# A fifth 2x2 problem in the FFN, and two output groups that share PSUM banks

## The chip, the cores and the metric

The kernel runs on one core of one Trainium2 chip. The metric is device time in microseconds of one execution, 1881.71 us before the change (median of 3 runs, 1881.66 to 1881.78).

## The reference

Two layers of a post-norm encoder over 512 tokens of width 1024, in float32. Each layer has a token mixer (retention, chunked attention and differential attention, gated, merged and projected) and a SwiGLU FFN with 2816 inner columns. The change is in the FFN:

```python
u = jnp.einsum('bsd,df->bsf', x, w_ffn_in[l])
u_gate, u_up = jnp.split(u, 2, axis=-1)
ffn = jnp.einsum('bsf,fd->bsd', jax.nn.silu(u_gate) * u_up, w_ffn_out[l])
x = _layer_norm(DEEPNORM_ALPHA * x + ffn, ln2_g[l], ln2_b[l])
```

## The kernel before, in words

**Numbers.** A float32 operand is carried as a pair of float32r, high and low. ACT casts the high part and DVE subtracts to get the low part. A product of two pairs is three matmuls (`mm3`, L121 to L124). Weights are loaded in blocks of 1 MB into four staging buffers (`st`, queue SP); ACT casts `wh` (L259, plain blocks L154) and DVE subtracts `wl` (L260, L155) into three pairs of weight buffers (`AHEAD`, L48). A staging buffer is free for the next load when its `wl` is done.

**2x2 problems.** Most of the FFN's products are done as 2x2 block problems with seven products (m1, m2, y, x, v, g, h) in place of eight, each of 24 matmuls of 512 columns. The weight sums that they need come about in two ways. A `Chain` (L193) adds the next block of weights onto the one in the staging buffer by an accumulating DMA, which is issued by POOL (`more`, L178) after that buffer was split. A `Close` adds staged blocks with DVE (L233, L239) and needs one accumulating DMA ahead (`ahead_a`). Both load the block for g ahead of time: a plain load and, when it has landed, an accumulating one onto it (`ahead_c`). Written "p m1" and so on: problem p, product m1.

**FFN, first part.** The 22 inner tiles of 128 columns are made from x1, the layer-norm of the mixer's output, turned (`x1T`: eight pairs of 128 rows by 512 tokens). Four problems p, q, r, u (`u_fin`, L1272) make tiles 0 to 15: p is a Chain, the others are Closes. Tiles 16 to 21 are plain (`u_ffn`, `u_ffn_first`); 16 and 17 run first, on the first 256 tokens and then on the rest, because the last tokens' layer-norm is not yet through. `Quarters.sums` makes the sums of x1T (`s_x1`), and `s_natural` makes the untransposed x1 on DVE. `s_turn` transposes the gated results back (eight PE transposes each, L1222).

**FFN, second part.** Two output groups o and w (`fout_items`, L1307) are Chains over hidden tiles 0 to 7 and 8 to 15. The left-hand sums are made by `Twins`: `ready` (m1, m2), `difference` (y), `sums` (x, v), `rest` (g, h), each a DVE operation or none and a split. Each product stands in PSUM for the two row blocks (j = 0, 1), and DVE adds it into z (`plus`, L1303) for each of o and w. Products x, g and h of a group accumulate onto the bank of m1, and v onto that of y. `fout_rest(0)` and `fout_rest(1)` add the products of the six plain tiles 16 to 21; the second runs to the layer's end with the layer-norm behind it.

**Order.** The items of the FFN stand in a list written by hand (L1364 to L1376). With each item stand groups of side work, which are run between the halves of the item. A scheduler orders the instructions of each engine when the kernel is built; on the chip every engine's queue runs in order.

Of the kernel before, what the change touches and what calls it, by code (L numbers as in the profile page):

```python
# [17 lines left out]
P = 128  # L18
# [3 lines left out]
KT = D // P  # L22
# [34 lines left out]
def trunk(ctx, tc, x_in, xT_in, w_in, ret_norm_g, da_norm_g, lq1, lk1, lq2, lk2, w_a, w_b, w_c, b_merge, w_out,  # L57
# [19 lines left out]
    def g(dt=F32, name="g"):  # L77
        return gp.tile([P, 512], dt, tag="g", name=name)
# [4 lines left out]
    def bank(name="ps"):  # L83
        return psp.tile([P, 512], F32, tag="ps", name=name)

    class Pair:


        def __init__(self, name="pr"):
            self.hi = g(F32R, name + "h")  # L90
            self.lo = g(F32R, name + "l")

    class HalfPair:

# [21 lines left out]
    def split(pr, src, cols=slice(None), scale=None):  # L116

        part_hi(pr.hi[:, cols], src, scale)
        part_lo(pr.lo[:, cols], src, pr.hi[:, cols], scale)

    def mm3(ps, lh, ll, rh, rl, start, stop, onto=False):  # L121
        nc.tensor.matmul(ps, lh, rh, start=start, stop=False, skip_group_check=onto)  # L122
        nc.tensor.matmul(ps, lh, rl, start=False, stop=False, skip_group_check=onto)  # L123
        nc.tensor.matmul(ps, ll, rh, start=False, stop=stop, skip_group_check=onto)  # L124
# [137 lines left out]
    class Quarters:  # L262
# [13 lines left out]
        def put(self, name, pr, sl):  # L276
            self.use[name] = pr.hi[:, sl], pr.lo[:, sl]

        def sums(self, t1, t2, scale=None):
            a, b = self.A, self.B  # L280
            sa, sb = g(name="sa"), g(name="sb")
            nc.vector.tensor_sub(sa[:, a], t1[:, b], t2[:, b])
            nc.vector.tensor_sub(sa[:, b], sa[:, a], t1[:, a])
            nc.vector.tensor_add(sb[:, a], t2[:, a], sa[:, b])
            nc.vector.tensor_sub(sb[:, b], t1[:, a], t1[:, b])
            p12, p43 = Pair("s12"), Pair("s43")
            split(p12, sa, scale=scale)
            split(p43, sb, scale=scale)
            for name, pr, sl in (("y", p12, a), ("x", p12, b), ("v", p43, a), ("g", p43, b)):
                self.put(name, pr, sl)  # L290

    class Twins:

# [33 lines left out]
        def rest(self):  # L327
            nc.vector.tensor_sub(self.a21, self.a11, self.a21)
            self.part("g", self.a21)
            self.part("h", self.a22)  # L330

    def product(acts, name, j, wt, ps=None):

# [26 lines left out]

    def proj_N(act, wts, t, ps, k0=0, start=True, stop=True):

        sl = slice(P * t, P * t + P)
        rows = [(wt, k) for wt in wts for k in range(wt.nk)]
        for i, (wt, k) in enumerate(rows):
            a = act[k0 + i]
            mm3(ps, a.hi[:, sl], a.lo[:, sl], wt.hi[:, k], wt.lo[:, k], start and i == 0, stop and i == len(rows) - 1)

    def rows_of(w, c, k0=0, nk=KT):

# [232 lines left out]
    def layer(l):  # L603
# [118 lines left out]
        def s_q(k):  # L722

            def fn():
                xq[k].sums(xf.pop(k), xf.pop(k + 4))
            return fn

        def u_two(hv, acts, left_done, right_done):
# [433 lines left out]
        def u_out1(*wts):  # L1162
            n = x1["n"]
            for t in range(NT):
                ps = bank("po")
                proj_N(mg, wts, t, ps)
                if t >= 1:
                    n.transposes(t - 1)
                residual(n.z[t][1], ps)
                n.stats(t, 1)  # L1170
                n.normalise(t)
                if t == 2:
                    n.to_T(0)

        banks0 = []
        for i in range(2):
# [49 lines left out]

        twins = {}

        def s_ready(gi, fp):
            def fn():  # L1230
                pa, pc, k = 2 * gi, 2 * gi + 1, 8 * gi + 2 * fp
                tw = twins[gi, fp] = Twins(half.pop((pa, 0, fp)), half.pop((pa, 1, fp)))
                tw.ready(half.pop((pc, 0, fp)))
                hid[k], hid[k + 1] = tw.each
            return fn

        def s_differ(gi, fp):
# [9 lines left out]
        def s_rest(gi, fp):  # L1247
            def fn():
                twins.pop((gi, fp)).rest()
            return fn  # L1250

        def s_hid(*ids):
# [6 lines left out]
        def s_x1(k):  # L1259
            def fn():  # L1260
                if k == 0:
                    x1q.update({i: Quarters(x1T[i], x1T[i + 4]) for i in range(4)})
                x1q[k].sums(x1f.pop(k), x1f.pop(k + 4))
            return fn

        def s_natural(*ts):
# [10 lines left out]
        def u_ffn_first(ids):  # L1277
            def fn(*wts):
                n = len(ids)
                pg, pu = [bank("pt") for _ in range(n)], [bank("pt") for _ in range(n)]  # L1280
                proj_T_half0(x1T, [(wts[i], P * j, p[i]) for i in range(n) for j, p in enumerate((pg, pu))],
                             {KT // 2: lambda: (x1["n"].transposes(3), x1["n"].to_T(1))})
                for i in range(n):
                    proj_T(x1T, wts[i], 0, ps=pg[i], half=1)
                    proj_T(x1T, wts[i], P, ps=pu[i], half=1)
                    ffn_done(ids[i], pg[i], pu[i])
            return [ffn_spec(i) for i in ids], fn

        def u_ffn(i):
            def fn(wt):  # L1290
# [13 lines left out]
            if final:  # L1304
                x2["n"].stats(t, hf)

        def fout_items(gi):  # L1307

            r0, kh = GROUPS[gi]
            hv = Chain(w_ffn_out[l], r0, kh)  # L1310
            w = {}

            def it(name, *adds):
# [12 lines left out]

            add, sub = ALU.add, ALU.subtract
            return {"c": hv.ahead_c, "m1": it("m1", (0, 0, add)), "y": it("y", (1, 1, add)), "x": it("x", (0, 1, sub)),
                    "m2": it("m2", (0, 0, add)), "v": it("v", (0, 1, add)), "g": it("g", (1, 1, sub)), "h": it("h", (1, 0, add))}

        def fout_rest(hf):

# [31 lines left out]
        for (specs, fn), *groups in [  # L1364
            (u_ffn_first([16, 17]), [s_natural(0)], [s_x1(0)]), (p["m1"], [s_x1(1)], [s_x1(2)]),
            (u_ffn(18), [s_x1(3), s_natural(1)], [p["c"]]), (p["m2"], [s_natural(2)], [s_natural(3)]), (p["y"],),
            (p["v"], [q["a"]]), (u_ffn(19),), (p["x"],), (q["m1"],), (p["g"],), (q["y"], [s_turn(0, 0)]), (p["h"], [q["c"]]),
            (q["v"], [r["a"]]), (q["m2"], [s_turn(0, 1)]), (q["x"],), (r["m1"],), (q["g"],), (r["y"], [s_turn(1, 0)]), (q["h"], [r["c"]]),
            (r["v"], [u["a"]]), (r["m2"], [s_turn(1, 1)]), (r["x"],), (u["m1"],), (r["g"],), (u["y"], [s_turn(2, 0)]),
            (r["h"], [u["c"]], [s_ready(0, 0)]), (u["v"], [s_ready(0, 1)]), (u["m2"], [s_turn(2, 1)]), (u["x"],),  # L1370
            (o["m1"], [s_differ(0, 0)], [s_differ(0, 1)]), (u["g"],), (o["m2"], [s_sums(0, 0)], [o["c"]]), (u["h"], [s_turn(3, 0)]),
            (o["y"], [s_sums(0, 1)]), (u_ffn(20), [s_rest(0, 0)], [s_rest(0, 1)]), (o["v"], [s_turn(3, 1)]),
            (o["x"], [s_ready(1, 0)], [s_ready(1, 1)]),
            (w["m1"], [s_differ(1, 0)]), (o["g"], [s_differ(1, 1)], [w["c"]]), (w["m2"], [s_sums(1, 0)]), (o["h"], [s_sums(1, 1)]),
            (w["y"], [s_rest(1, 0)]), (u_ffn(21), [s_rest(1, 1)], [s_hid(16, 17, 18)]), (w["v"], [s_hid(19, 20, 21)]), (w["x"],),
            (fout_rest(0),), (w["g"],), (w["h"],), (fout_rest(1),),  # L1376
        ]:
            item(specs, fn, *groups)

# [58 lines left out]
```

## Time and profile before

| | us |
|---|---|
| median of 3 runs | 1881.71 |
| the profiled execution | 1881.89 |
| its span, first to last instruction | 1880.1 |
| PE busy | 1865.1 (99%) |
| DVE busy | 1353.0 (72%) |
| ACT busy | 974.2 (52%) |
| POOL busy | 119.2 (6%) |

Times in rows are microseconds from the span's start. A row of the timeline gives start, duration, engine, line, operation, output and inputs, and in brackets the idle time before it and what ended it. A row of the waits gives who waited for whom: us in total, times, longest. A group's row gives the busy time and the mean duration in ns, then the idle time of the engine ahead of it. A table of stretches gives the busy time of each engine in each stretch. The granted TensorE clock was 0.999 over the span.

### The profile page before, as it was taken

What the parts mean: (1) busy time and instruction counts of PE and PEld (TensorE: products, weight loads), DVE (VectorE), ACT (ScalarE), POOL (GpSimd) and SP (SyncE); (2) the same over time, 40 slices, a digit from 0 to 9 for tenths busy, and PEclk for the clock granted to TensorE, in tenths of its full rate; (3) what the DMA queues carried; (4) which work ended last, traced back from release to release, by engine and by line L of the source; (5) the groups of instructions that cost most, each with busy time, mean ns of one, the idle gap of its engine ahead of it and who ended that gap; (6) DMA issues with size and microseconds to landing.
All of it is one profiled execution on the core that took longest, in us unless ns stands there. A gap on an engine that the chain in (4) does not pass through costs nothing. (4 is left out here: it accounts for less than half of the span.)

```text
span 1880.1 us, 23994 instructions
## 1 busy us (share of the span) xinstructions
PE 1865.1 (99%) x9138; PEld 1572.9 (84%) x9138; DVE 1353.0 (72%) x2059; ACT 974.2 (52%) x1579; POOL 119.2 (6%) x145
## 2 busy tenths in 40 slices
PE   9999999999999999999999999999999999999998
PEld 7888888888888888888898888888888888888886
DVE  6767756667766867888687778566776668678886
ACT  5545545567643545554355546455766344455541
POOL 2000000000001000010010000000000010000100
PEclk9999999999999999999999999999999999999999
DMA  9585443332145667787375944533322556777871
GB/s 287 163 278 151 123 146 124 108 118 89 57 160 153 159 190 189 196 223 197 124 200 166 288 112 130 168 114 105 123 68 65 195 132 174 178 195 204 201 192 45
DMA packets 219795, 295.59 MB, mean 157 GB/s; under 512 B 8484, under 2 KB 115072, under 8 KB 219680
## 3 DMA queue, kind: packets, MB, share of 16 engines
q1 hardware_dynamic: 193568, 243.30, 38.9%
q0 software_dynamic: 26112, 50.76, 15.7%
q8 instruction: 72, 1.18, 0.3%
q14 instruction: 43, 0.35, 0.1%
HBM read 270.90 MB, written 23.12 MB: 156 GB/s over the span
## 5 line engine op out<-in xcount | busy, mean ns | idle before, releaser
L122 PE MATMUL pt<-xTh,wh 128*128 128x512 f32 (+1 forms) x1072 | 396.8, 371 | 1.6 <-ACT wh L154 1.6
L123 PE MATMUL pt<-xTl,wh 128*128 128x512 f32 (+1 forms) x1072 | 393.5, 367 | 1.9 <-DVE xTl L112 1.9
L124 PE MATMUL pt<-xTh,wl 128*128 128x512 f32 (+1 forms) x1072 | 393.6, 368 | 0.0
L260 DVE TENSOR_TENSOR wl<-st,wh 128x2048 fp32r<-128x2048 f32 x126 | 288.1, 2289 | 126.3 <-ACT wh L259 118.8
L259 ACT CAST wh<-st 128x2048 fp32r<-128x2048 f32 x126 | 240.6, 1912 | 182.7 <-PE pf L124 116.8
L155 DVE TENSOR_TENSOR wl<-st,wh 128x1024 fp32r<-128x1024 f32 (+1 forms) x204 | 218.6, 1094 | 64.5 <-ACT wh L154 54.3
L154 ACT CAST wh<-st 128x1024 fp32r<-128x1024 f32 (+1 forms) x204 | 188.0, 948 | 139.6 <-issue 55.2
L123 PEld LDWEIGHTS pt<-xTl,wh 128*128 128x128 f32 x1072 | 202.3, 189 | 34.2 <-DVE xTl L112 2.3
L124 PEld LDWEIGHTS pt<-xTh,wl 128*128 128x128 f32 x1072 | 202.0, 189 | 33.7
L122 PEld LDWEIGHTS pt<-xTh,wh 128*128 128x128 f32 x1072 | 201.9, 189 | 33.8 <-ACT wh L154 2.1
L122 PE MATMUL pf<-wh,xTh 128*128 128x512 f32 x336 | 131.9, 393 | 1.1 <-ACT rph L106 0.8
L123 PE MATMUL pf<-wl,xTh 128*128 128x512 f32 x336 | 130.9, 390 | 0.0
L124 PE MATMUL pf<-wh,xTl 128*128 128x512 f32 x336 | 130.8, 389 | 0.0
L745 ACT COPY tc<-pf 128x512 f32<-128x512 f32 x84 | 48.4, 587 | 78.4 <-PE pf L124 73.0
L122 PE MATMUL pf<-wh,s12h 128*128 128x512 f32 x224 | 88.0, 393 | 0.0
L122 PE MATMUL pf<-wh,s43h 128*128 128x512 f32 x224 | 87.6, 391 | 0.1
L123 PE MATMUL pf<-wl,s12h 128*128 128x512 f32 x224 | 87.3, 390 | 0.0
L124 PE MATMUL pf<-wh,s43l 128*128 128x512 f32 x224 | 87.2, 389 | 0.0
L123 PE MATMUL pf<-wl,s43h 128*128 128x512 f32 x224 | 87.2, 389 | 0.0
L124 PE MATMUL pf<-wh,s12l 128*128 128x512 f32 x224 | 87.2, 390 | 0.0
L122 PEld LDWEIGHTS pf<-wh,xTh 128*128 128x128 f32 x336 | 63.1, 188 | 15.7 <-ACT rph L106 1.6
L124 PEld LDWEIGHTS pf<-wh,xTl 128*128 128x128 f32 x336 | 63.1, 188 | 13.2
(317 smaller groups left out, 3706.9 us busy)
## 6 DMA issues: line engine op xcount, KB each, us to landing
st<-in_w_in SPq DMA_DIRECT2D x60, 1024.0 KB, 5.2
st<-in_w_ffn_in SPq DMA_DIRECT2D x38, 1024.0 KB, 5.2
st<-in_w_ffn_in POOLq DMA_DIRECT2D x20, 1024.0 KB, 10.4
st<-in_w_ffn_out SPq DMA_DIRECT2D x20, 1024.0 KB, 8.1
st<-in_w_in SPq DMA_DIRECT2D x32, 512.0 KB, 5.1
st<-in_w_ffn_out POOLq DMA_DIRECT2D x16, 1024.0 KB, 9.0
st<-in_w_in POOLq DMA_DIRECT2D x12, 1024.0 KB, 11.3
th<-th SPq DMA_DIRECT2D x48, 256.0 KB, 4.7
```

Of the source, the lines that this page charges most:

```text
L122: nc.tensor.matmul(ps, lh, rh, start=start, stop=False, skip_group_check=onto)
L123: nc.tensor.matmul(ps, lh, rl, start=False, stop=False, skip_group_check=onto)
L124: nc.tensor.matmul(ps, ll, rh, start=False, stop=stop, skip_group_check=onto)
L154: return [nc.scalar.copy(self.hi[:, a:b], self.st[:, a:b]), nc.vector.tensor_sub(self.lo[:, a:b], self.st[:, a:b], f(self.hi[:, a:b]))]
L155: nc.vector.tensor_sub(self.lo[:, a:b], self.st[:, a:b], f(self.hi[:, a:b]))]
L259: nc.scalar.copy(self.hi, st)
L260: nc.vector.tensor_sub(self.lo, st, f(self.hi))
L745: nc.scalar.copy(t[to, j], ps)
```

## The change

- Inner tiles 16 to 19 become a fifth problem e, a Chain on weight columns 2048 to 2559 of each half. Its m1 and m2 come first, behind the mixer, and p becomes a Close. Tiles 20 and 21 stay plain and follow; `u_ffn_first` with its halves of 256 columns is gone.
- `Quarters.sums` is cut into `left` (y, x) and `right` (v, g); `Twins.ready` into `first` (m1) and `second` (m2), so that their parts can stand at different places of the list.
- e's turned results are read by the rest products through `Across`, since their two row blocks lie in two pairs.
- o and w go product by product, and both accumulate in the same banks: a product of w is added onto o's in PSUM, and only w's are added to z. x, g and h of o then accumulate onto a bank that holds w's last product.
- The list is written anew. FFN-out's order is now o m1, w m1, o m2, w m2, o y, w y, rest(0), o v, w v, o x, w x, o g, w g, o h, w h, rest(1), with u g and u h among the first of them.

```diff
-        def sums(self, t1, t2, scale=None):
+        def left(self, t1, t2):
...
+        def right(self, t1, t2):
...
-        def ready(self, a12):
+        def first(self):
+            self.part("m1", self.a11)
+
+        def second(self, a12):
             self.a12 = a12
-            self.part("m1", self.a11)
             self.part("m2", a12)
...
+        def s_across(fp):
+            def fn():
+                prs = []
+                for hf in range(2):
+                    prs.append(Pair("hid"))
+                    split(prs[hf], half.pop((4, hf, fp)))
+                for i in range(2):
+                    hid[REST + 2 * fp + i] = Across(prs, i)
             return fn
...
                     for j in range(2):
-                        w[on, j] = product([hid[r0 + k] for k in range(kh)], name, j, wt, w.pop((on, j), None))
-                        for i, hf, op in adds:
-                            plus(2 * i + j, hf, w[on, j], op, gi == 1 and name == "h")
-                        if name in ("m2", "v", "h"):
-                            w.pop((on, j))
-                return [getattr(hv, name)], fn
+                        w[on, j] = product([hid[r0 + k] for k in range(kh)], name, j, wt, w.get((on, j)))
+                        for i, hf, op in adds if gi else ():
+                            plus(2 * i + j, hf, w[on, j], op, name == "h")
+                        between()
+                return [getattr(hvs[gi], name)], fn
...
-        p, q, r, u = u_fin(0, Chain), u_fin(1, Close), u_fin(2, Close), u_fin(3, Close)
-        o, w = fout_items(0), fout_items(1)
+        e, p, q, r, u = [u_fin(pb, kind) for pb, kind in ((4, Chain), (0, Close), (1, Close), (2, Close), (3, Close))]
+        o, w = fout_items()
         for (specs, fn), *groups in [
-            (u_ffn_first([16, 17]), [s_natural(0)], [s_x1(0)]), (p["m1"], [s_x1(1)], [s_x1(2)]),
-            (u_ffn(18), [s_x1(3), s_natural(1)], [p["c"]]), (p["m2"], [s_natural(2)], [s_natural(3)]), (p["y"],),
-            (p["v"], [q["a"]]), (u_ffn(19),), (p["x"],), (q["m1"],), (p["g"],), (q["y"], [s_turn(0, 0)]), (p["h"], [q["c"]]),
+            (e["m1"], [], [s_turned]), (e["m2"], [s_x1(0, 1)], [s_x1(2, 3)]), (u_ffn(20), [s_natural(0), e["c"]], [s_x1r(0, 1)]),
+            (u_ffn(21), [s_x1r(2, 3), s_natural(1)], [p["a"]]), (e["y"], [s_natural(2)]), (e["v"], [s_natural(3)]), (p["m1"],), (e["x"],),
+            (p["y"],), (e["g"], [s_turn(4, 0)], [p["c"]]), (p["v"],), (e["h"], [q["a"]]), (p["m2"], [s_turn(4, 1)]), (p["x"],),
+            (q["m1"],), (p["g"],), (q["y"], [s_turn(0, 0)]), (p["h"], [q["c"]]),
...
-            (w["m1"], [s_differ(1, 0)]), (o["g"], [s_differ(1, 1)], [w["c"]]), (w["m2"], [s_sums(1, 0)]), (o["h"], [s_sums(1, 1)]),
-            (w["y"], [s_rest(1, 0)]), (u_ffn(21), [s_rest(1, 1)], [s_hid(16, 17, 18)]), (w["v"], [s_hid(19, 20, 21)]), (w["x"],),
-            (fout_rest(0),), (w["g"],), (w["h"],), (fout_rest(1),),
+            (o["y"], [s_differ(1, 0)], [s_differ(1, 1)]), (w["y"], [s_across(0)], [s_across(1), s_hid(20, 21)]),
+            (fout_rest(0), [s_sums(0, 0)], [s_sums(0, 1)], [s_sums(1, 0)], [s_sums(1, 1)]),
+            (o["v"], [o["c"]]), (w["v"], [w["c"], s_rest(0, 0)], [s_rest(0, 1)]), (o["x"], [s_rest(1, 0)], [s_rest(1, 1)]), (w["x"],),
+            (o["g"],), (w["g"],), (o["h"],), (w["h"],), (fout_rest(1),),
```

More of the change, by code (lines that the diff above doesn't have):

```diff
@@ L91, in __init__, with at @@
             self.lo = g(F32R, name + "l")
+        def at(self, t):
+            return self.hi[:, P * t:P * t + P], self.lo[:, P * t:P * t + P]
     class HalfPair:
@@ L277, in put @@
             self.use[name] = pr.hi[:, sl], pr.lo[:, sl]
-        def sums(self, t1, t2, scale=None):
+        def left(self, t1, t2):
             a, b = self.A, self.B
[L281 to L290, printed above, removed]
+            s = self.s = g(name="sa")
+            nc.vector.tensor_sub(s[:, a], t1[:, b], t2[:, b])
+            nc.vector.tensor_sub(s[:, b], s[:, a], t1[:, a])
+            pr = Pair("s12")
+            split(pr, s)
+            self.put("y", pr, a)
+            self.put("x", pr, b)
+        def right(self, t1, t2):
+            a, b = self.A, self.B
+            s = g(name="sb")
+            nc.vector.tensor_add(s[:, a], t2[:, a], self.s[:, b])
+            nc.vector.tensor_sub(s[:, b], t1[:, a], t1[:, b])
+            pr = Pair("s43")
+            split(pr, s)
+            self.put("v", pr, a)
+            self.put("g", pr, b)
     class Twins:
@@ L330, in rest, with __init__, at @@
             self.part("h", self.a22)
+    class Across:
+        def __init__(self, halves, i):
+            self.halves, self.i = halves, i
+        def at(self, t):
+            pr, o = self.halves[t // 2], 256 * self.i + P * (t % 2)
+            return pr.hi[:, o:o + P], pr.lo[:, o:o + P]
     def product(acts, name, j, wt, ps=None):
@@ L361, in proj_N @@
     def proj_N(act, wts, t, ps, k0=0, start=True, stop=True):
-        sl = slice(P * t, P * t + P)
         rows = [(wt, k) for wt in wts for k in range(wt.nk)]
         for i, (wt, k) in enumerate(rows):
-            a = act[k0 + i]
-            mm3(ps, a.hi[:, sl], a.lo[:, sl], wt.hi[:, k], wt.lo[:, k], start and i == 0, stop and i == len(rows) - 1)
+            hi, lo = act[k0 + i].at(t)
+            mm3(ps, hi, lo, wt.hi[:, k], wt.lo[:, k], start and i == 0, stop and i == len(rows) - 1)
     def rows_of(w, c, k0=0, nk=KT):
@@ L724, in fn @@
             def fn():
-                xq[k].sums(xf.pop(k), xf.pop(k + 4))
+                t1, t2 = xf.pop(k), xf.pop(k + 4)
+                xq[k].left(t1, t2)
+                xq[k].right(t1, t2)
             return fn
@@ L1173, in u_out1 @@
                     n.to_T(0)
+            x1q.update({i: Quarters(x1T[i], x1T[i + 4]) for i in range(4)})
         banks0 = []
@@ L1227, in layer, with s_first, s_second @@
         twins = {}
-        def s_ready(gi, fp):
+        def s_first(gi, fp):
             def fn():
-                pa, pc, k = 2 * gi, 2 * gi + 1, 8 * gi + 2 * fp
+                pa, k = 2 * gi, 8 * gi + 2 * fp
                 tw = twins[gi, fp] = Twins(half.pop((pa, 0, fp)), half.pop((pa, 1, fp)))
-                tw.ready(half.pop((pc, 0, fp)))
+                tw.first()
                 hid[k], hid[k + 1] = tw.each
+            return fn
+        def s_second(gi, fp):
+            def fn():
+                twins[gi, fp].second(half.pop((2 * gi + 1, 0, fp)))
             return fn
@@ L1250, in s_rest, with fn @@
             return fn
+        def s_across(fp):
+            def fn():
+                prs = []
[4 more added lines that the diff above has]
+                    hid[REST + 2 * fp + i] = Across(prs, i)
+            return fn
         def s_hid(*ids):
@@ L1257, in s_hid, with s_turned, s_x1, s_x1r @@
             return fn
-        def s_x1(k):
+        def s_turned():
+            x1["n"].transposes(3)
+            x1["n"].to_T(1)
+        def s_x1(*ks):
             def fn():
-                if k == 0:
-                    x1q.update({i: Quarters(x1T[i], x1T[i + 4]) for i in range(4)})
-                x1q[k].sums(x1f.pop(k), x1f.pop(k + 4))
+                for k in ks:
+                    x1q[k].left(x1f[k], x1f[k + 4])
+            return fn
+        def s_x1r(*ks):
+            def fn():
+                for k in ks:
+                    x1q[k].right(x1f.pop(k), x1f.pop(k + 4))
             return fn
@@ L1275, in u_fin @@
                          functools.partial(gate_half, pb), functools.partial(gated, pb))
[L1277 to L1287, printed above, removed]
         def u_ffn(i):
@@ L1305, in plus, with fout_items, it @@
                 x2["n"].stats(t, hf)
-        def fout_items(gi):
-            r0, kh = GROUPS[gi]
-            hv = Chain(w_ffn_out[l], r0, kh)
+        def fout_items():
+            hvs = [Chain(w_ffn_out[l], r0, kh) for r0, kh in GROUPS]
             w = {}
-            def it(name, *adds):
+            def it(gi, name, *adds):
+                r0, kh = GROUPS[gi]
                 def fn(wt):
@@ L1319, in fn @@
                     for j in range(2):
-                        w[on, j] = product([hid[r0 + k] for k in range(kh)], name, j, wt, w.pop((on, j), None))
-                        for i, hf, op in adds:
-                            plus(2 * i + j, hf, w[on, j], op, gi == 1 and name == "h")
-                        if name in ("m2", "v", "h"):
-                            w.pop((on, j))
-                return [getattr(hv, name)], fn
+                        w[on, j] = product([hid[r0 + k] for k in range(kh)], name, j, wt, w.get((on, j)))
[3 more added lines that the diff above has]
+                return [getattr(hvs[gi], name)], fn
             add, sub = ALU.add, ALU.subtract
-            return {"c": hv.ahead_c, "m1": it("m1", (0, 0, add)), "y": it("y", (1, 1, add)), "x": it("x", (0, 1, sub)),
-                    "m2": it("m2", (0, 0, add)), "v": it("v", (0, 1, add)), "g": it("g", (1, 1, sub)), "h": it("h", (1, 0, add))}
+            adds = {"m1": (0, 0, add), "y": (1, 1, add), "x": (0, 1, sub), "m2": (0, 0, add), "v": (0, 1, add),
+                    "g": (1, 1, sub), "h": (1, 0, add)}
+            return [{"c": hvs[gi].ahead_c, **{name: it(gi, name, a) for name, a in adds.items()}} for gi in range(2)]
         def fout_rest(hf):
@@ L1368, in layer @@
             (q["v"], [r["a"]]), (q["m2"], [s_turn(0, 1)]), (q["x"],), (r["m1"],), (q["g"],), (r["y"], [s_turn(1, 0)]), (q["h"], [r["c"]]),
             (r["v"], [u["a"]]), (r["m2"], [s_turn(1, 1)]), (r["x"],), (u["m1"],), (r["g"],), (u["y"], [s_turn(2, 0)]),
-            (r["h"], [u["c"]], [s_ready(0, 0)]), (u["v"], [s_ready(0, 1)]), (u["m2"], [s_turn(2, 1)]), (u["x"],),
-            (o["m1"], [s_differ(0, 0)], [s_differ(0, 1)]), (u["g"],), (o["m2"], [s_sums(0, 0)], [o["c"]]), (u["h"], [s_turn(3, 0)]),
@@ L1372, in layer @@
-            (o["y"], [s_sums(0, 1)]), (u_ffn(20), [s_rest(0, 0)], [s_rest(0, 1)]), (o["v"], [s_turn(3, 1)]),
-            (o["x"], [s_ready(1, 0)], [s_ready(1, 1)]),
-            (w["m1"], [s_differ(1, 0)]), (o["g"], [s_differ(1, 1)], [w["c"]]), (w["m2"], [s_sums(1, 0)]), (o["h"], [s_sums(1, 1)]),
-            (w["y"], [s_rest(1, 0)]), (u_ffn(21), [s_rest(1, 1)], [s_hid(16, 17, 18)]), (w["v"], [s_hid(19, 20, 21)]), (w["x"],),
-            (fout_rest(0),), (w["g"],), (w["h"],), (fout_rest(1),),
+            (r["h"], [u["c"]]), (u["v"],), (u["m2"], [s_turn(2, 1)], [s_first(0, 0)]), (u["x"], [s_first(0, 1)]),
@@ new lines, in layer @@
+            (o["m1"],), (u["g"], [s_first(1, 0)], [s_first(1, 1)]), (w["m1"], [s_turn(3, 0)], [s_second(0, 0)]),
+            (u["h"], [s_second(0, 1)]), (o["m2"], [s_second(1, 0), s_second(1, 1)], [s_differ(0, 0)]), (w["m2"], [s_turn(3, 1)], [s_differ(0, 1)]),
+            (o["y"], [s_differ(1, 0)], [s_differ(1, 1)]), (w["y"], [s_across(0)], [s_across(1), s_hid(20, 21)]),
+            (fout_rest(0), [s_sums(0, 0)], [s_sums(0, 1)], [s_sums(1, 0)], [s_sums(1, 1)]),
+            (o["v"], [o["c"]]), (w["v"], [w["c"], s_rest(0, 0)], [s_rest(0, 1)]), (o["x"], [s_rest(1, 0)], [s_rest(1, 1)]), (w["x"],),
```

## The prediction

> **What bounds the kernel now.** I read the page's busy line first, then the waits of PE, then the stretches of the first layer's FFN (598 to 912 us; the second layer repeats its order).
>
> ```profile
> span 1880.1 us, 23994 instructions
> PE 1865.1 (99%) x9138; PEld 1572.9 (84%) x9138; DVE 1353.0 (72%) x2059; ACT 974.2 (52%) x1579; POOL 119.2 (6%) x145
> ```
>
> ```profile
> PE pt L123 <- DVE xTl L112: 1.9, 2, 1.0
> PE pt L122 <- ACT wh L154: 1.6, 1, 1.6
> PE warm L574 <- POOL ident masks.py:199: 1.5, 1, 1.5
> PE pf L122 <- ACT rph L106: 0.8, 2, 0.4
> ```
>
> PE is busy for 1865.1 of 1880.1 us and waits 5.8 us in all. So the time is the sum of PE's instructions plus its waits plus the tail after its last matmul, and a change can pay only by fewer or shorter matmuls. The next table (length, then busy time of PE, PEld, DVE, ACT, POOL; clock; DMA share; GB/s) shows how thin the cover is.
>
> ```profile
> 600.00:625.00 25.00, 24.04 (x199) 23.75 (x199) 15.31 (x30) 14.90 (x32) 3.23 (x3) 1.00 0.66 143
> 625.00:650.00 25.00, 25.00 (x112) 20.71 (x111) 23.77 (x37) 12.92 (x15) 1.29 (x1) 1.00 0.67 182
> 800.00:825.00 25.00, 25.00 (x116) 20.80 (x115) 23.16 (x29) 13.66 (x16) 2.56 (x2) 1.00 1.08 291
> 850.00:875.00 25.00, 25.00 (x112) 20.71 (x111) 24.25 (x29) 12.95 (x13) 1.28 (x1) 1.00 0.94 229
> ```
>
> PE never waits in the last three, yet DVE is busy for 23.16 to 24.25 of 25 us. DVE's queue is in order: work put into such a stretch reaches PE.
>
> **PE's own work.** Starts of single rows give the pitches:
>
> ```profile
> 574.91 0.39 PE L122 MATMUL po<-wh,mgh 128*128 128x512 f32 x1
> ...
> 585.80 1.03 PE L500 MATMUL px<-ident,z 128*128 128x128 f32 x8
> 586.59 0.48 PE L122 MATMUL po<-wh,mgh 128*128 128x512 f32 x1
> 586.90 0.40 PE L123 MATMUL po<-wl,mgh 128*128 128x512 f32 x1
> ...
> 600.83 0.28 PE L122 MATMUL pt<-xTh,wh 128*128 128x256 f32 x1
> ...
> 601.91 0.28 PE L122 MATMUL pt<-xTh,wh 128*128 128x256 f32 x1
> ...
> 603.63 0.39 PE L123 MATMUL pt<-xTl,wh 128*128 128x256 f32 x1 [0.96 <-DVE xTl L112]
> ```
>
> A 512-column matmul costs 10.89 / 48 = 0.227 us (574.91 to 585.80), a 256-column one 1.08 / 9 = 0.120, and eight transposes 0.79 plus 0.08 by which the next matmul is late, 0.87. Per layer the built order loses 96 full matmuls (tiles 18, 19) and 192 half ones (16, 17), and gains 7 x 24 = 168 full ones and 16 transposes: -21.8 - 23.0 + 38.1 + 1.7 = -5.0 us. The wait at 603.63 goes too, since e's m1 and m2 (written e m1, e m2), which come first now, need only the first 256 tokens: -1.0. So the work is worth -6.0 us a layer, and **with no new wait the run would take 1881.9 - 12 = 1869.9**. (Sums stand against the profiled execution, 1881.89 us; its span is 1.8 shorter, the median of the runs, 1881.71, 0.2 below.) The tail behind the last matmul is the same code; I count nothing for it.
>
> **DVE's work.** Durations:
>
> ```profile
> L260 DVE TENSOR_TENSOR wl<-st,wh 128x2048 fp32r<-128x2048 f32 x42 | 95.9, 2288 | 34.1 <-ACT wh L259 33.9
> L155 DVE TENSOR_TENSOR wl<-st,wh 128x1024 fp32r<-128x1024 f32 x12 | 14.3, 1219 | 0.8 <-ACT wh L154 0.8
> L112 DVE TENSOR_TENSOR xTl<-xf,xTh 128x256 fp32r<-128x256 f32 x13 | 5.0, 420 | 4.9 <-ACT xTh L106 4.9
> ```
>
> ```profile
> 849.50 0.69 DVE L1303 TENSOR_TENSOR z<-z,pf 128x512 f32<-128x512 f32 x1
> 850.11 0.69 DVE L317 TENSOR_TENSOR ta<-hf 128x512 f32<-128x512 f32 x1
> ...
> 851.49 2.29 DVE L260 TENSOR_TENSOR wl<-st,wh 128x2048 fp32r<-128x2048 f32 x1
> 853.70 0.68 DVE L1303 TENSOR_TENSOR z<-z,pf 128x512 f32<-128x512 f32 x1
> ```
>
> Start to start these are 2.21 (2048 wide) and 0.61 (512 wide, taken as 0.60), some 0.08 under the durations; by the same overlap I take 1.14 (1024) and 0.34 (256). Per layer DVE gets 7 more wide splits (+15.5), 8 fewer 1024 splits (-9.1), 2 more staged sums of p as Close (+4.4), 6 more tc additions (+3.6) and 14 fewer z additions, because o's products stay in PSUM (-8.4): about +6 us in 315, harmless on average. It matters where they stand. Below, times are those at which PE would be in the changed order if it never waited, counted in the pitches from 598 us.
>
> **Wait A, the start.** From 602.2, DVE's queue up to the low halves of e x's weights holds 4 wide splits, one of 1024, 21 operations of 512 and 17 of 256: 8.8 + 1.1 + 12.6 + 5.8 = 28.3 us, through 630.5. PE wants those weights at 631.7, so 1.2 us are to spare; but in this queue stands p m1's split as well. Its load goes out at 614.3, when a staging buffer is free, behind two accumulating loads of POOL. Such loads were:
>
> ```profile
> L174 SPq DMA_DIRECT2D st<-in_w_ffn_in x17: 367/368/384, 599.4 to 763.6; - x17
> ...
> DMA to landing us min/median/max: 4.9/5.7/10.8
> ```
>
> I take 9, nearer the slow end since two transfers are in flight: 623.3, plus 1.9 of ACT's cast and 2.2 of the split, 627.5. PE is to start on it at 626.0 (first wait 1.5), and behind it 8.4 us of DVE work are left before e x's weights are split, 635.9 against 631.7. **A = 4.2 us** in all; the load at 5.7 would make it 1.2, at 10.8 and more casts in the way 4.8.
>
> **Wait B, FFN-out's y products.** In the changed order both groups' y and both halves of the across tiles fall between 820 and 850 us. From 820.5 DVE owes 3 wide splits, two of 1024 and 34 operations of 512: 6.6 + 2.3 + 20.4 = 29.3 us, to 849.8; the last hidden low is wanted at 849.6. On top come casts of ACT that DVE waits for with nothing else in line, some two or three of 0.6. **B = 1.4 us**, bounds 0.2 and 3.
>
> **Wait C, the shared bank.** o g accumulates into the bank that w x's product has just filled, so PE must wait until DVE has added w x into z. Before, o and w had banks of their own and `fout_rest(0)` stood between. In DVE's queue that addition stands behind the split of w's c block (w g's weights), and that block comes late: its plain load goes out when w v's split has freed a buffer, at 860.0, and its accumulating load follows the landing.
>
> ```profile
> 804.28 1.28 POOL L178 DMA_DIRECT2D st<-in_w_ffn_out  x1 [16.51 <-DVE ta L317]
> 809.69 1.28 POOL L178 DMA_DIRECT2D st<-in_w_ffn_out  x1 [4.13 <-DVE wl L260]
> ...
> 848.24 1.28 POOL L178 DMA_DIRECT2D st<-in_w_ffn_out  x1 [10.36 <-DMA st<-in_w_ffn_out]
> ```
>
> ```profile
> 841.99 0.37 SPq L174 DMA_DIRECT2D st<-in_w_ffn_out  x1
> ```
>
> ```profile
> L178 POOL DMA_DIRECT2D st<-in_w_ffn_out x8: 1282/1282/1282, 786.5 to 875.8; - x8
> ...
> DMA to landing us min/median/max: 8.2/9.0/12.4
> ```
>
> The same hand-over at 841.99 took 6.25 us until POOL issued. So POOL issues at 866.3 with another accumulating load 3.4 us ahead of it; I take 10.8 us to landing, between the median and the slowest (the second of the pair at 804 and 809): 877.1. Cast 1.9, split 2.2, one split of 0.6 and the addition 0.7 bring it to 882.5; PE wants the bank at 878.6. **C = 3.9 us**; a landing of 8.2 makes it 1.3, and a plain load a little quicker too 0.5; 12.4 makes it 5.5.
>
> One page speaks against these prices. The Trainium skill, "DMA: Bandwidth & Descriptors", section "Anatomy of one DMA — SWDGE (gpsimd) path", fits a POOL-issued transfer as about 2.0 us plus its bytes over 436 GB/s, an estimate of 4.4 us for 1 MB. With that C would be nothing and the sum 7.8 us lower, 1881.2; but the fastest accumulating load here took 8.2, so the measurement decides.
>
> **Other edits.** A fourth wait, D, is possible: p m2's load goes out within half a microsecond of q's accumulating load near 649; landing in about 6 us it is in time, in 10.8 it delays p m2 and q m1 by about 4 us. I take 0, since the fast case is the median of the row above. Four more accumulating loads over both layers cost POOL 1.28 us each, beside its 6% busy. Splitting Quarters.sums and Twins.ready changes when, not what; it is in the queues counted above. The last z additions and the tail gain nothing, since PE sets their start.
>
> **Sum.** Per layer -6.0 + 4.2 + 1.4 + 3.9 = +3.5; two layers +7.0; 1881.9 + 7.0 = **1888.9 us, slower by 0.37%**.
>
> **Rivals.**
> - *No new wait holds* (ends faster): the plain loads land in 5.7 and the accumulating ones in 8.2 to 9, and A, B and C stay near their lower ends, 1.2 + 0.2 + 0.5 = 1.9: per layer -4.1, 1873.7; with none at all 1869.9. For it: PE did not starve in stretches where DVE was busy for 24.25 of 25. Against: C's chain is one late transfer and needs no crowd. It decides at 6.0 us of new waits a layer.
> - *Only one of A and C is real*: -6.0 + 4 + 1.4 = -0.6 a layer, or 1880.7: no change.
> - *D comes too*: +4.1 a layer more, 1897.
> - *The clock falls.* Every stretch above has a granted clock of 1.00, and the longest wait of PE there was 1.6 us; A and C are longer. If matmuls ran at half speed after such a wait for as long as it lasted, each wait would cost half of itself again: 4 us a layer, 1897. The Trainium skill states such a rule in "TensorE: Matmul & The Clock Gate", section "What's actually happening": a free-running window of some 3.4 us without activity halves the clock. No run so far shows it; A comes in two pieces, and a wait of 3.9 us rarely covers a whole window, so I give it little.
> - That the change leaves the matmul count as it was is excluded by the built order: 208 fewer of 9138 over both layers.
>
> **How the numbers follow.** Forecast (A, B and C, 1882 to 1893) 0.50; no or small waits (1870 to 1877) 0.20; only one of them 0.15; D as well 0.10; the clock 0.05. 0.2% of the time, 3.8 us, is about what a measurement can tell from no change: same is 1878.0 to 1885.5. Faster: the second case and a little of the third, 0.22. Same: the rest of the third and a lower part of the first, 0.20. Slower 0.58. The range leaves out no new wait at all below and the sum of all upper ends (4.8 + 3 + 5.5 + 4.1 - 6.0 = 11.4 a layer, 1904.7) above: 1873 to 1898.
>
> **What would show it.** PE's waits in the changed profile should name `wl` and the load behind it around 626 to 637 us, hidden splits around 840 to 850, and `z` around 879 to 884, each again in the second layer some 935 us on, and PE's busy time should fall by about 10 us. If PE's waits stay under 6 us in all, A, B and C were wrong together; if the wait at the bank is there but short, the accumulating load was quicker than 10.8; if PE's busy time does not fall, the pitch was wrong.

## The result and the profile after

The changed kernel takes 1907.34 us (median of 4 runs, 1906.49 to 1908.50) against 1881.68 us: ratio 1.0137, 95% interval [1.0119, 1.0154]. It is slower, as forecast, but by 25.7 us and not by 7; the time lies 9 us above the range. The profiled execution took 1908.5 us.

The first lines of the page:

```profile
span 1906.7 us, 23567 instructions
PE 1871.2 (98%) x8930; PEld 1560.3 (82%) x8930; DVE 1365.2 (72%) x2045; ACT 995.5 (52%) x1597; POOL 124.4 (7%) x149
```

PE has 208 instructions fewer, worth 10 us by the pitches, and yet is busy for 6 us more. So its matmuls became slower somewhere. The waits of PE (us in total, times, longest):

```profile
PE pf L125 <- DVE z L1339: 10.4, 2, 5.3
PE pf L126 <- DVE wl L263: 5.9, 5, 1.8
PE pt L125 <- ACT wh L157: 2.8, 3, 1.3
PE pf L125 <- ACT wh L262: 1.5, 2, 0.8
PE pf L127 <- DVE qm2l L115: 1.5, 3, 0.9
```

The names are those that the prediction gave: z at the shared bank (C), weights at the start (A). The two stretches in which they lie, in the first layer (length, busy time of PE, PEld, DVE, ACT, POOL; clock; DMA share; GB/s):

```profile
640.00:665.00 25.00, 21.46 (x84) 16.66 (x84) 22.62 (x29) 13.71 (x15) 1.28 (x1) 0.93 0.54 147
...
890.00:915.00 25.00, 19.72 (x76) 15.82 (x75) 14.51 (x16) 8.23 (x8) 1.83 (x2) 0.86 0.96 220
```

The granted clock is 0.93 and 0.86 here, where it was 1.00 in every stretch of the kernel before that the prediction shows. PE's rows show what that is. Wait A, at p m1:

```profile
640.95 0.49 PE L125 MATMUL pf<-wh,xTh 128*128 128x512 f32 x1 [0.80 <-ACT wh L262]
643.28 0.50 PE L126 MATMUL pf<-wl,xTh 128*128 128x512 f32 x1 [1.83 <-DVE wl L263]
643.61 0.43 PE L127 MATMUL pf<-wh,xTl 128*128 128x512 f32 x1
643.84 0.63 PE L125 MATMUL pf<-wh,xTh 128*128 128x512 f32 x1
644.27 0.63 PE L126 MATMUL pf<-wl,xTh 128*128 128x512 f32 x1
...
647.26 0.40 PE L127 MATMUL pf<-wh,xTl 128*128 128x512 f32 x1
647.49 0.40 PE L125 MATMUL pf<-wh,xTh 128*128 128x512 f32 x1
```

From 643.84 to 647.26 eight matmuls start 0.427 us apart, not 0.227: 1.6 us lost after the wait is over. These 1.6 us do not lengthen the layer by themselves, though. DVE stood idle until p m1's weights came; from p m1's split to e x's split its queue then holds 8.48 us of work without a pause, and PE cannot start on e x's low halves before that:

```profile
640.93 2.29 DVE L263 TENSOR_TENSOR wl<-st,wh 128x2048 fp32r<-128x2048 f32 x1 [4.71 <-ACT wh L262]
...
649.41 2.29 DVE L263 TENSOR_TENSOR wl<-st,wh 128x2048 fp32r<-128x2048 f32 x1
```

```profile
651.75 0.50 PE L126 MATMUL pf<-wl,s12h 128*128 128x512 f32 x1 [0.91 <-DVE wl L263]
```

Experiment 2 shows the same start of e x without slow matmuls ahead of it. Wait C, at o g:

```profile
907.83 0.77 PE L125 MATMUL pf<-wh,qgh 128*128 128x512 f32 x1 [5.28 <-DVE z L1339]
908.40 0.63 PE L126 MATMUL pf<-wl,qgh 128*128 128x512 f32 x1
...
913.51 0.39 PE L126 MATMUL pf<-wl,qgh 128*128 128x512 f32 x1
913.74 0.40 PE L127 MATMUL pf<-wh,qgl 128*128 128x512 f32 x1
```

Twelve slow starts from 908.40 to 913.51: 5.11 - 12 x 0.227 = 2.4 us. What released C is the chain that the prediction walked: POOL's loads first, then ACT, then DVE.

```profile
886.83 1.28 POOL L181 DMA_DIRECT2D st<-in_w_ffn_out  x1 [10.89 <-DVE wl L263]
889.25 1.29 POOL L181 DMA_DIRECT2D st<-in_w_ffn_out  x1 [1.15 <-issue]
890.81 1.28 POOL L181 DMA_DIRECT2D st<-in_w_ffn_out  x1 [0.27 <-DVE wl L263]
```

```profile
902.26 1.90 ACT L262 CAST wh<-st 128x2048 fp32r<-128x2048 f32 x1 [7.05 <-DMA st<-in_w_ffn_out]
```

```profile
904.20 2.29 DVE L263 TENSOR_TENSOR wl<-st,wh 128x2048 fp32r<-128x2048 f32 x1 [6.43 <-ACT wh L262]
906.40 0.68 DVE L115 TENSOR_TENSOR qgl<-hf,qgh 128x512 fp32r<-128x512 f32 x1
907.01 0.68 DVE L1339 TENSOR_TENSOR z<-z,pf 128x512 f32<-128x512 f32 x1
```

The load of 889.25 landed after 12.9 us, with one accumulating load 2.4 us ahead of it and one 1.6 us behind it. In the same way p m1's plain load, issued at 627.9 behind two accumulating loads (621.4 and 622.9), took 11.0 us.

Where the 26.6 us between the two profiled executions are, by the starts of PE's matmuls (a wait is what a gap has over the pitch, both layers together):

| term | forecast | measured |
|---|---|---|
| matmuls and transposes, counts times pitch | -10.0 | -10.1 |
| the old wait at the FFN's start | -2.0 | -2.2 |
| A | +8.4 | +8.2 |
| B | +2.8 | +3.3 |
| C | +7.8 | +11.4 |
| slow matmuls behind A and C (1.6, 2.4, 1.6, 2.2) | 0 | +7.7 |
| waits in the mixer | 0 | +2.9 |
| transposes ahead of the FFN | 0 | +1.0 |
| gaps under 0.25 us each | 0 | +4.4 |
| sum | +7.0 | +26.6 |

### The profile page after: what moved, and what is told of

Its sections match the earlier page's. It is cut to its first block, busy times and chain, and to the rows that moved or that the text cites. A ratio compares the mean times of both kernels' runs of the same rounds, so it can differ in the third digit from the quotient of the medians.

```text
span 1906.7 us, 23567 instructions
## 1 busy us (share of the span) xinstructions
PE 1871.2 (98%) x8930; PEld 1560.3 (82%) x8930; DVE 1365.2 (72%) x2045; ACT 995.5 (52%) x1597; POOL 124.4 (7%) x149
## 5 line engine op out<-in xcount | busy, mean ns | idle before, releaser
L263 DVE TENSOR_TENSOR wl<-st,wh 128x2048 fp32r<-128x2048 f32 x140 | 320.4, 2291 | 156.6 <-ACT wh L262 155.6
L262 ACT CAST wh<-st 128x2048 fp32r<-128x2048 f32 x140 | 267.8, 1915 | 200.8 <-PE pf L127 111.3
L125 PE MATMUL pt<-xTh,wh 128*128 128x512 f32 (+1 forms) x880 | 335.6, 383 | 3.0 <-ACT wh L157 2.8
L126 PE MATMUL pt<-xTl,wh 128*128 128x512 f32 (+1 forms) x880 | 332.4, 378 | 0.0
L127 PE MATMUL pt<-xTh,wl 128*128 128x512 f32 (+1 forms) x880 | 332.3, 378 | 0.0
L125 PEld LDWEIGHTS pt<-xTh,wh 128*128 128x128 f32 x880 | 165.5, 188 | 33.7 <-ACT wh L157 4.1
L127 PEld LDWEIGHTS pt<-xTh,wl 128*128 128x128 f32 x880 | 165.4, 188 | 31.3
L126 PEld LDWEIGHTS pt<-xTl,wh 128*128 128x128 f32 x880 | 165.7, 188 | 29.4
L126 PE MATMUL pf<-wl,xTh 128*128 128x512 f32 x384 | 151.5, 395 | 4.0 <-DVE wl L263 4.0
L126 PEld LDWEIGHTS pf<-wl,xTh 128*128 128x128 f32 x384 | 72.9, 190 | 19.9 <-DVE wl L263 5.4
```

The lines of the kernel that those rows point to most:

```text
L262: nc.scalar.copy(self.hi, st)
L263: nc.vector.tensor_sub(self.lo, st, f(self.hi))
```

## The experiments

**1. The mixer's sums as before.** In `s_q` alone, `left` and `right` are replaced by the old method, which makes all sums and then splits.

```diff
-                xq[k].left(t1, t2)
-                xq[k].right(t1, t2)
+                xq[k].sums(t1, t2)
```

> The changed kernel (1907.3 us) with one edit undone: in the mixer, Quarters.sums makes all four sums first and splits them afterwards, as before; the FFN keeps left and right. Theory: the new waits of PE in the mixer (1.0 us near 80 us of the span, 2.0 us near 1019 to 1029) come from the split order alone; they go and the time falls by 3 us, to 1904.3. Rival: they come from the FFN's other demands on the queues (in layer 1) and from a shifted load (in layer 0); then at least the 2.0 us of layer 1 stay and the time falls by 1 us or less, 1906.3 to 1907.5.

Measured 1905.62 us (1901.97 to 1906.46). PE waits for nothing between 70 and 90 us nor between 1000 and 1040 in this profile. The waits go in both layers, so the order of the splits made them. The fall in time, 1.7 us, is less sharp than the rows, since the waits in the FFN vary from run to run; experiment 10 measures it with those gone.

**2. o g in fresh banks.**

```diff
                     for j in range(2):
+                        if name == "g" and gi == 0:
+                            w["old", j] = w.pop((on, j))
                         w[on, j] = product([hid[r0 + k] for k in range(kh)], name, j, wt, w.get((on, j)))
                         for i, hf, op in adds if gi else ():
+                            if name in ("g", "h"):
+                                plus(2 * i + j, hf, w["old", j], op)
                             plus(2 * i + j, hf, w[on, j], op, name == "h")
```

> The changed kernel with o g started in two fresh banks, so that PE need not wait for w x's additions to z; for products g and h DVE adds the old bank too (8 more z additions in all). Theory: the wait at o g (5.3 and 5.3 us) was only the shared bank behind a late accumulating load, and the slow matmuls behind it (2.4 and 2.2 us more than at full clock) follow from the wait; both go, minus about 15 us, 1892; up to 3 us may come back as waits for o h's weights, whose accumulating load lands at 909.3 in the profile. Rival 1: the late load holds PE just as long at o g's second half or w g, since the weights themselves are late: 1904 or more. Rival 2: the slow matmuls stay without the wait: minus 10.5, 1897.

Measured 1898.36 us (1897.43 to 1901.33), 9.0 less. The wait at o g is gone, and in the first layer the slow matmuls with it:

```profile
890.00:915.00 25.00, 23.58 (x105) 19.18 (x103) 19.95 (x23) 11.53 (x11) 2.59 (x2) 1.00 0.99 227
```

The late load still lands late: its split ends at 905.1, where PE is at o g from 902.5. It holds PE only through the bank. What came back was not o h's weights but the same thing one product on: o h accumulates onto the bank of w g, whose addition stands behind w h's split. PE waits there for z again, 1.6 us and 3.8 us more than the pitch, the second with slow matmuls behind it (1.4 us).

This profile also tells what the slow matmuls behind A cost. In its first layer none follow the wait at p m1; instead PE waits 2.51 us at e x, where it was 0.91:

```profile
642.29 0.50 PE L126 MATMUL pf<-wl,xTh 128*128 128x512 f32 x1 [1.82 <-DVE wl L263]
...
650.77 0.50 PE L126 MATMUL pf<-wl,s12h 128*128 128x512 f32 x1 [2.51 <-DVE wl L263]
```

From the one row to the other are 8.48 us, as in the changed kernel (643.28 to 651.75). It is 8.47 or 8.48 us in all eight layers of the four profiles with wait A (the changed kernel, experiments 1, 2 and 4), with slow matmuls in between or without. So e x's start is set by DVE's queue, and the slow matmuls behind p m1 only fill time in which PE would have stood.

**3. p's ahead block one item later.**

```diff
-            (u_ffn(21), [s_x1r(2, 3), s_natural(1)], [p["a"]]), (e["y"], [s_natural(2)]),
+            (u_ffn(21), [s_x1r(2, 3), s_natural(1)]), (e["y"], [s_natural(2)], [p["a"]]),
```

> The changed kernel with p's ahead block (a plain and an accumulating load) asked for one item later, behind p m1's load instead of ahead of it. Theory: the wait A at p m1 was p m1's plain load, issued at 627.9 while two accumulating loads ran and landing after 11.0 us; it now goes out some 10 us sooner, the waits at p m1 (2.9 us a layer) and the slow matmuls after them (1.6 us a layer) go, and most of the 1.0 us at e x: minus 9 to 11 us, 1897. Rival: A is a DVE queue that is full; then p m1 waits as long for its split as before and the time stays within 2 us of 1907.3.

Measured 1898.27 us (1895.26 to 1900.30), 9.1 less, as the theory said. Part of it is another gain: wait C is 1.4 us shorter in the first layer of this profile. The two plain loads that now go out at 618.6 and 629.4 land after 5.3 and 5.8 us, PE does not wait at p m1 in either layer, and the clock stays up:

```profile
640.00:665.00 25.00, 23.71 (x105) 19.29 (x104) 23.79 (x31) 12.38 (x13) 1.28 (x1) 1.00 0.82 216
```

The wait at e x stays (1.45 us over the pitch a layer).

**4. PE kept busy through wait C.** Half a product that nothing reads, ahead of o g. The edit calls `product` for one row block only, so it adds 12 matmuls a layer (2.7 us), where the expectation counts 24 (5.4 us). They are extra work and change no output.

```diff
+                    if name == "g" and gi == 0:
+                        product([hid[r0 + k] for k in range(kh)], name, 0, wt)
                     for j in range(2):
```

> The changed kernel with 24 useless matmuls of 512 columns (5.4 us, into a scratch bank that nothing reads) put into PE's queue ahead of o g in each layer; the wait for the shared bank is untouched, PE only works through it. Theory: the half clock after o g comes from PE standing idle; with PE busy the slow matmuls there go, minus 4.5 us, plus up to 0.4 where 5.4 us of work overruns the wait: 1903. Rival: the slow stretch has another cause (the loads in flight, or the wait's release), it stays, and the time is 1907.3 to 1908.

Measured 1902.04 us (1899.32 to 1903.36): 5.3 us less with 5.4 us more work. PE reaches the bank, works through the extra matmuls and stands for 1.05 us (0.93 in the second layer):

```profile
902.24 0.39 PE L125 MATMUL pf<-wh,qgh 128*128 128x512 f32 x1
...
904.73 0.39 PE L127 MATMUL pf<-wh,qgl 128*128 128x512 f32 x1
906.16 0.50 PE L125 MATMUL pf<-wh,qgh 128*128 128x512 f32 x1 [1.05 <-DVE z L1339]
906.50 0.39 PE L126 MATMUL pf<-wl,qgh 128*128 128x512 f32 x1
906.73 0.39 PE L127 MATMUL pf<-wh,qgl 128*128 128x512 f32 x1
```

Behind 1.05 us of standing the matmuls are 0.23 us apart, where they were 0.43 behind 5.28, with the same loads in flight. So the half clock comes from PE's standing idle. The wait itself was not untouched: the bank came 3.9 and 3.8 us after PE reached it, not 5.4 and 5.3, because the load ahead of it landed after 9.8 and 11.5 us in this profile. So some 3 us of the fall are not the clock's. That does not weaken the reading: in experiments 1 and 3 PE stands 3.97 and 3.88 us at the same place, unfilled, and slow matmuls follow both.

**5. All repairs at once**: 1 and 3, and o g and o h each in fresh banks (DVE adds the banks of x, g and h to z one by one).

> The changed kernel with all the repairs at once: the mixer's sums as before, p's ahead block one item later, and both o g and o h in fresh banks (DVE adds the banks of x, g and h to z one by one). Theory: the waits at p m1, o g and o h and the half clock behind them are the whole loss; from 1907.3 fall about 3 (mixer), 9 (p m1), 9 (o g) and 5 to 7 (o h in the kernel with o g alone repaired: 1.6 and 3.8 us of waits, 1.4 of slow matmuls): 1879.5 to 1881.5, no slow matmul left in the FFN. Rival: PE now meets w h's weights, whose accumulating load lands after 17 to 19 us, and stands again with a half clock behind it: 1886 or more.

Measured 1879.36 us (11 runs, 1877.49 to 1880.23), ratio 0.9988, interval [0.9979, 0.9997], just faster than the kernel before. The waits left in the FFN are B and e x's, none is long, and no slow matmul is left there:

```profile
PE pf L126 <- DVE wl L263: 2.6, 2, 1.3
...
PE pf L125 <- ACT qyh L109: 1.0, 2, 0.5
...
PE pf L127 <- DVE qm2l L115: 0.7, 2, 0.4
```

**6. The untransposed rows later as well.** `s_natural(0)` to `(3)` move behind e x, to e x, p y and e g, on top of 5.

> As the kernel with all repairs, and x1's untransposed rows (s_natural, 16 operations of DVE) are made four to six items later, behind e x's split. Theory: the wait that is left at e x (1.45 us a layer with p's block later) is DVE's crowded queue: it goes, minus 2.9 us against the kernel with all repairs, about 1877. Rival: it is the accumulating load of e x's weights; then the wait stays and the time is the same within 1 us; or the rows crowd p y's and e g's splits and as much comes back there.

Measured 1892.22 us (1890.05 to 1893.22), 13 us worse than 5. The wait at e x did go, so it was DVE's crowded queue. But the rows now stand ahead of p m2's split, p's staged sum and p x's split, which frees the buffer for q m1's load. That load goes out later:

```profile
680.21 1.28 POOL L181 DMA_DIRECT2D st<-in_w_ffn_in  x1 [11.26 <-DMA st<-in_w_ffn_in]
```

```profile
683.67 0.38 SPq L177 DMA_DIRECT2D st<-in_w_ffn_in  x1
```

Behind the accumulating load by 3.5 us, it lands after 9.9 us. With all repairs alone it goes out at 678.8, within 0.2 us of the accumulating load (678.9), and lands after 5.6. So 4.9 us of delay at the issue become 9.2 at the landing, and PE waits 4.5 us for the casts (and 1.2 us at p x before) and has eleven slow starts behind them. This is the mechanism of the prediction's wait D, one load further on; the change itself escaped it. The theory of the queue held, its time did not.

**7. Stops of PE in the kernel before.** A chain of copies on ACT behind products x and h, and a transpose that waits for it. No load is late there.

```diff
+    def stop(ps, n):
+        t = g(name="idl")
+        nc.scalar.copy(t, ps)
+        for _ in range(n):
+            nc.scalar.copy(t, t)
+        px = bank("idp")
+        tc.keep_in_program_order(nc.tensor.transpose(px[:, :P], t[:, :P], ident))
```

> The kernel before, with PE made to stand at 14 places of the FFN behind products x and h: a chain of 2 to 9 copies on ACT and a transpose that waits for it, 1.3 to 5.5 us each. Nothing else is late there. Theory: standing alone drops the clock: behind stops of more than about 3 us the matmuls of 512 columns start 0.43 us apart in place of 0.227 for some 2.5 to 5 us; behind stops under 2 us they do not; in between it depends on where the stop falls. Rival: the half clock belongs to the loads in flight at the start and in FFN-out; then no slow matmul follows any of the stops and only the standing itself is added.

Measured 1985.81 us (one run). The stops came out at 2.7 to 7.5 us, longer than meant, and all 14 are followed by slow matmuls, 1.0 to 2.3 us over the pitch each, 1.7 on the mean.

**8. Shorter stops**, copies of 64 columns.

> As the kernel of the 14 stops, the copies 64 columns wide: 1.2 to 2.8 us of standing each. In the kernel of the longer stops all 14 (2.9 to 7.7 us) were followed by slow matmuls. Theory: there is a bound between 2.0 us (the longest stop in the other runs with no slow matmul behind it) and 2.7 us (the shortest with them), near it decided by where the stop falls: none of the stops under 2 us is followed by slow matmuls, some of those over 2.3 us are. Rival: the price falls with the length and has no bound: short stretches follow the short stops too.

Measured 1939.35 us (one run). Two stops side by side, with the matmuls that follow:

```profile
767.76 0.30 PE L130 MATMUL idp<-ident,idl 128*64 128x128 f32 x1 [3.07 <-ACT idl L128]
767.81 0.48 PE L134 MATMUL pf<-wh,xTh 128*128 128x512 f32 x1
768.13 0.39 PE L138 MATMUL pf<-wl,xTh 128*128 128x512 f32 x1
768.36 0.39 PE L139 MATMUL pf<-wh,xTl 128*128 128x512 f32 x1
...
817.56 0.34 PE L130 MATMUL idp<-ident,idl 128*64 128x128 f32 x1 [2.25 <-ACT idl L128]
817.61 0.72 PE L134 MATMUL pf<-wh,qm1h 128*128 128x512 f32 x1
818.13 0.63 PE L138 MATMUL pf<-wl,qm1h 128*128 128x512 f32 x1
818.55 0.63 PE L139 MATMUL pf<-wh,qm1l 128*128 128x512 f32 x1
```

A stop of 2.25 us is followed by eight slow starts, one of 3.07 by none. Over both kernels: three stops of 0.3 to 0.9 us, no slow matmul; nine of 2.25 to 3.15, slow behind seven; sixteen of 3.35 and more, slow behind all. So the length decides at both ends, and between 2.2 and 3.2 us it does not decide alone; that it depends on where the stop falls fits this, but is not shown. The price grows a little with the length: 1.3 us on the mean behind the seven shorter stops, 1.8 behind the sixteen longer ones. Stops between 1.0 and 2.2 us were not made here, but the other changed kernels have fourteen single waits of 1.0 to 1.8 us, and no slow matmul follows any of them. Two waits with one matmul between them, as in A (0.3 to 0.8 and 1.8 us), are followed by slow matmuls in six of the eight layers that have them.

**9. The rows only one or two items later** (the first stays, e x's stretch loses four operations), on top of 5.

> As the kernel with all repairs (1879.4 us), and x1's untransposed rows made one or two items later only (the first stays): four operations of DVE leave the stretch ahead of e x's split, and the rows end ahead of p m2's load. Theory: the wait at e x (1.45 us a layer) loses up to 2.4 us of DVE work ahead of it and goes, and p m2's load still leaves close behind q's accumulating load: minus 2.9 us, 1876.5. Rival: the rows push the staged sum that frees p m2's buffer so late that its load falls 3 us behind the accumulating load, as with the rows four to six items later (landing after 9.9 in place of 5.6 us): 1886 to 1892.

Measured 1880.63 us (12 runs, 1874.17 to 1883.51), ratio 0.9984 [0.9973, 0.9995]: no different from 5 within its runs. In the profiled one the wait at e x is gone in both layers, and in the second layer q m1 waits (1.8 us; the load in question is q m1's, where the expectation names p m2's). Its load goes out 0.7 us ahead of the accumulating one in the first layer and lands after 5.6 us; in the second it goes out 2.5 us behind and lands after 9.0. So the cliff of 6 is near enough to be met in one layer and not in the other: the theory holds for e x in both layers, the rival for the load in one. A wait of 1.6 us for m2's low half in the second layer takes more of the gain.

**10. All repairs but the mixer's.**

> The kernel with all repairs (1879.4 us, ratio 0.9988) without the repair in the mixer: the sums of xT are split left and right as in the change. Theory: the split order in the mixer costs its waits, 0.9 us in the first layer and 2.0 in the second, whatever else is repaired: 1882.3, ratio to before 1.0003. Rival: with the FFN repaired the mixer's waits move into slack, and the time is that of all repairs within 1 us.

Measured 1882.76 us (1881.31 to 1887.11), ratio 1.0007 [0.9998, 1.0016], against 1879.36 with it: the split order in the mixer costs 3.4 us, the theory's 2.9 within the spread.

## Why the prediction was wrong

- *PE's own work*, -6.0 us a layer: right (-5.0 of counts, -1.1 of the old wait); with the counts and the pitches the table closes. DVE's work, +6 a layer, was right too: its busy time went from 1353.0 to 1365.2 us over both layers.
- *Wait A*, 4.2 a layer: right in its mechanism, too small in size. p m1's load, behind two accumulating ones, took 11.0 us where 9 was taken, and 8.48 us of DVE's work (8.4 taken) carried the delay on to e x. PE lost 3.0 us at p m1 and 2.7 up to e x (1.1 of waiting, 1.6 of slow matmuls inside it), 5.7 a layer. Moving the load left 1.45 of it. The table's +8.2 looks like a hit only because the slow matmuls have a row of their own.
- *Wait B*, 1.4: right in size (1.1 and 2.2). The rows name other operands than the forecast: m2's low halves (`qm2l`) and ACT's cast for y (`qyh`); no split of a hidden tile holds PE.
- *Wait C*, 3.9: the mechanism was right step by step, the size was not: 5.8 and 5.6. The mis-sized term is the landing of w's c block, 12.9 us where 10.8 was taken. The third accumulating load (890.81), which was not counted, does not explain it: a third one runs in all nine profiles with this order, and the second takes 9.8 to 10.3 us where it goes out 3.8 to 4.1 us behind the first (five layers) and 11.5 to 13.8 where it goes out 2.0 to 2.8 us behind (thirteen). Here it was 2.4 (2.1 in the second layer), and 3.4 was taken. The standing itself was 5.3 us, at the upper bound given (5.5, for a landing of 12.4).
- *The clock*, at nothing in the sum: the step that failed. The prediction had it as a rival with its price, 4 us a layer, and gave it 0.05 with the words that A comes in two pieces and a wait of 3.9 us rarely covers a whole window. It was there in both layers behind both waits, 7.7 us of slow matmuls. Those behind A ran in time that PE would have stood at e x; those behind C, 4.5 us, are the clock's own cost. The stops show that an idle time over about 2.2 us risks it, and all sixteen of 3.35 us and more had it. By these rows a C of 3.9 us brings the half clock with it, so it belonged into the sum. That the price, half of the wait again, comes near the 7.7 is luck: behind stops of 2.3 to 7.5 us it is 1.0 to 2.4 us and does not go in proportion.
- *Splitting Quarters.sums "changes when, not what"*, at nothing: failed. The same method serves the mixer, where the splits now stand ahead of the second half's sums in the queues of ACT and DVE; it cost 2.9 us, and 3.4 by experiment 10. The FFN's lists had been walked and the mixer's had not.
- *The range* was missed for these together: A 3.0 with the slow matmuls inside it, C 3.6, the clock behind C 4.5, the mixer 2.9, and 5.4 of transposes and small gaps that were not counted.
- *Two slips that changed nothing.* The times named inside the FFN are some 14 us early: PE is at p m1 at 640.0, not at 626.0, since 168 matmuls (38 us) stand between e m1's start at 600.3 and it. The load shifted as much (627.9 for 614.3), so the wait stays. And 7.8 us below 1888.9 is 1881.1, not 1881.2.
- What stays open: of the 4.4 us of small gaps, I have not told apart which lie behind waits (the first matmuls after one are 0.3 us apart) and which are shifted loads. Why the mixer's waits differ between the layers was not tried either.

## What to carry to other kernels

Where PE is busy for 99% of the span, price every new wait of PE over 2 us with the slow matmuls that follow it, here 1.3 us on the mean behind stops of up to 3.2 us and 1.8 behind longer ones. Leave the price out where PE would have to wait soon after anyway. A shared accumulator saves additions, but it ties PE to the reader's queue: look at what stands ahead of the read there, above all a split that waits for a load. When a method is cut in two, walk the order of every caller.

## What the runs showed of the hardware

- TensorE at half pace after standing: 0.427 us for 0.227 us a matmul, for 2.1 to 5.1 us, behind 23 of 25 stops of 2.25 us and more and behind none of three under 1 us. The Trainium skill, "TensorE: Matmul & The Clock Gate", section "What's actually happening", speaks of a free-running window of about 3.4 us without activity that halves the clock. The halving agrees (0.427 for 0.227), but stops of 2.25 and 2.52 us sufficed here, and so did an idle time broken by a single matmul (0.80 and 1.83).
- Loads of 1 MB that share the DMA engines: what counts is when a plain one is issued. In the changed kernel's profile the five issued within 0.5 us behind an accumulating load took 5.6 to 6.1 us; the eight issued 1.4 to 3.0 us behind one took 9.8 to 11.3 us and landed 0.8 to 1.6 us after it. p m1's, 6.5 and 5.0 us behind two, took 11.0 us. Three accumulating ones within 4 us took 8.2, 12.9 and 18.5 us. The Trainium skill, "DMA: Bandwidth & Descriptors", section "Issuing engines are not separate DMA queues", has it that such loads run on the same engines and interleave; loads that slow each other, as here, agree with that. That a plain load a few us behind an accumulating one lands only after it is what these runs add; why, they do not show.
